# Moving three groups of matmul operands by 64 to 224 bytes in SBUF: a two-block transformer forward pass on one core

## The chip, the core and the metric

The program runs on one core of one Trainium2 chip. The metric is device time in microseconds (us) for one launch. Three runs of the kernel before gave 4149.29, 4153.81 and 4155.1 us; the median, 4153.81 us, is the time before.

## The reference

Two transformer-like blocks follow one another on 256 tokens of width 2048, all in fp32. The first block mixes tokens with two attention branches (a latent-attention branch and a sparse branch with an indexer), the second with an mLSTM and a small state-space model; each then has the same kind of feed-forward part, a product-key memory ("peer"): every token picks 16 of 128 x 128 = 16384 experts per head, for 8 heads.

```python
x = x + merged @ w_out                                   # block 1, after the two branches
x = x + peer_ffn(rmsnorm(x, g), w_q, sub_keys, u, v)     # experts' u and v: 16384 x 2048 each
x = rmsnorm(x, norm_final_g)
...                                                      # block 2: the same frame, another mixer
u = u_emb[expert]
a = gelu(einsum('thkd,td->thk', u, xb))
coef = (softmax(top_scores) * a)
out = einsum('thk,thkd->td', coef, v_emb[expert])
```

## The kernel before

The kernel computes the feed-forward parts densely: all 16384 expert activations are formed by matrix products with all of `u`, multiplied by a gate matrix that is zero where an expert was not picked, and multiplied with all of `v`. Every large product is done in three matmuls of type fp32r, because each operand is split into a high part and a low remainder: high x high, high x low, low x high. `products` (line 231) issues all of them.

A matmul has a stationary operand (`lhsT`, 128 x 128, brought in by a weight load) and a moving operand (`rhs`) that is streamed past it. Two arrangements occur.

- *The U stages* (lines 551 to 570, `cols`): 128 weight tiles of each feed-forward part. The stationary operand is a 128 x 128 piece of `w_hi` or `w_lo`; the moving one is 256 columns of `hT`, the normalised activations, transposed and split (`norm_T`, line 301, writes them and `hT`, line 295, allocates them). 48 matmuls a tile, into `ps_u`. The query projections of both feed-forward parts and most input projections of the two mixers have the same shape.
- *The V stages* (`tile_v`): 128 weight tiles of each feed-forward part. The stationary operand is a piece of `coef_hi` or `coef_lo`, the gated activations; the moving one is 512 columns of `w_hi` or `w_lo`. 24 matmuls a tile, into `ps_v`. Both output projections (`out_proj`) and some input projections (`row_products`, `lead_products`) are of this kind, with a piece of `hT` or `ckvT` as the stationary operand.

Matmuls follow one another without a gap in the work; each weight load runs while the matmul before it streams.

SBUF is handed out by pools, in the order in which `Ctx` opens them: `const`, `small`, `state`, `weights`, `pairs` from the bottom, and two pools from the top (`side="right"`), `pad3` and `hT`; each stage opens its own pool (`mix1`, `route`, `mix2`) above `pairs`. In the program before, the tiles of interest begin at these bytes of each partition; what counts below is the remainder by 512, the length of one weight load's row (128 columns of 4 bytes).

| tile | begins at byte | by 512 |
|---|---|---|
| `w_hi`, four buffers | 67584, 71680, 75776, 79872 | 0 |
| `w_lo`, four buffers | 83968, 88064, 92160, 96256 | 0 |
| `coef_hi`, `coef_lo` (pool `pairs`) | 100352, 102400; 104448, 106496 | 0 |
| stage pools (`mix1`, `route`, `mix2`) | 108544 | 0 |
| `cqT`, `o_hi`, `o_lo` (pool `mix1`, behind its own pad of 32 bytes) | between 108576 and 141344 | 32 |
| `ckvT` (pool `mix1`) | 160832 | 64 |
| `hT` with shift 8 (input of both mixers and both feed-forward parts) | 196096 + 32 | 32 |
| `hT` with shift 0 (output projections) | 196096 | 0 |

All steps from one matmul of a tile to the next are multiples of 512 bytes for a stationary operand and of 1024 or 2048 for a moving one (`in_kv` and `in2_v` with their 272 and 344 columns apart), so the remainder of a tile holds for every matmul that reads it.

DMA loads go through SP's queue into `w_raw`, ScalarE (ACT) makes `w_hi`, VectorE (DVE) and in part GpSimd (POOL) make `w_lo`. Side work (routing, attention, the state-space model) is threaded between weight tiles by `step`.

Of the kernel before, what the change touches and what calls it, by code (L numbers as in the profile page):

```python
# [7 lines left out]
F32, F32R, F16, U32, I32 = dt.float32, dt.float32r, dt.float16, dt.uint32, dt.int32  # L8
# [4 lines left out]
P = 128  # L13
T = 256
TB = 2
D = 2048
KD = D // P
# [5 lines left out]
class Halves:  # L23


    def __init__(self, tiles, h):
        self.tiles, self.h = tiles, h
# [6 lines left out]
class Ctx:  # L34


    def __init__(self, ctx, tc):
        self.tc, self.nc = tc, tc.nc
        nc = self.nc
        pool = lambda name, bufs, **kw: ctx.enter_context(tc.tile_pool(name=name, bufs=bufs, **kw))  # L40
        self.const = pool("const", 1)
        self.small = pool("small", 1)
        self.state = pool("state", 1)
        self.wp = pool("weights", 2)
        self.two = pool("pairs", 2)
        self.pad3 = pool("pad3", 1, side="right")
        self.top = pool("hT", 1, side="right")
        nc.gpsimd.memset(self.pad3.tile([P, 112], F32, name="pad"), 0.0)
        self.ps = pool("psum", 2, space=bass.MemoryType.PSUM)
        it = self.const.tile([P, P], F32, name="iota_f")  # L50
        nc.gpsimd.iota(it, pattern=[[1, P]], base=0, channel_multiplier=-1,
                       allow_small_or_imprecise_dtypes=True)
        self.diff = it
        self.ident = self.const.tile([P, P], F32, name="ident")
        nc.vector.tensor_scalar(self.ident, it, 0.0, None, op0=OP.is_equal)
        self.iota = self.const.tile([P, P], F16, name="iota_h")
        nc.gpsimd.iota(self.iota, pattern=[[1, P]], base=0, channel_multiplier=0,
                       allow_small_or_imprecise_dtypes=True)
        self.half_pi = self.const.tile([P, 1], F32, name="half_pi")
        nc.vector.memset(self.half_pi, float(np.pi / 2))  # L60
        self.x = self.state.tile([P, TB, D], F32, name="x")
        self.sq = self.small.tile([P, TB, 4], F32, name="x_sq")
        self.sq2 = self.small.tile([P, TB, 4], F32, name="x_sq2")
        self.twice, self.first, self.normed, self.done, self.fused = False, {}, {}, set(), {}
        self.bg = []
        self.late = []
        self.credit = 0.0
        self.fine = 0
        self.last = None
        self.lo = [None, None]  # L70
        self.hold = False
# [222 lines left out]

    def hT(self, shift=8):

        both = self.top.tile([P, 2 * KD * T + 8], F32R, name="hT")[:, shift:shift + 2 * KD * T]
        both = both.rearrange("p (two k t) -> p two k t", two=2, k=KD)
        return both[:, 0], both[:, 1]

    def norm_T(self):

        with self.tc.high_priority(SOON):
            hh, hl = self.hT()
            for tb in range(TB):
                n = self.normed.pop(tb)
                tt = slice(tb * P, (tb + 1) * P)
                for c in range(4):
                    ps = self.ps.tile([P, 4, P], F32, name="ps_v", bufs=4)
                    for j in range(4):  # L310
                        self.nc.tensor.transpose(ps[:, j], n[:, (4 * c + j) * P:(4 * c + j + 1) * P], self.ident)  # L311
                    kk = slice(4 * c, 4 * c + 4)
                    split = self.split(hh[:, kk, tt], hl[:, kk, tt], ps)
        if self.twice:
            def scale():
                for tb in range(TB):
                    with self.behind(split):
                        r = self.rsqrt(self.first[tb], 1.0 / D)
                    for c in range(4):
                        o = self.x[:, tb, c * 512:(c + 1) * 512]  # L320
                        with self.behind(split):
                            self.nc.vector.tensor_scalar(o, o, r, None, op0=OP.mult)
                        yield 0.4

            self.bg.append(scale())
            self.twice = False
        return hh, hl
# [13 lines left out]
def peer(K, wq, keys, u, v, g_out, g_next=None, dst=None, later=None):  # L341
# [8 lines left out]
    nc, ctx = K.nc, ExitStack()  # L350
# [2 lines left out]
    rp = ctx.enter_context(K.tc.tile_pool(name="route", bufs=1))  # L353
    kt = rp.tile([P, keys.shape[1], P], F32, name="keysT", tag="acts", bufs=4)
    nc.gpsimd.dma_start(kt, keys)
    hh, hl = K.norm_T()

    i1T = rp.tile([P, T], F32, name="i1T")
    i2T = rp.tile([P, T], F16, name="i2T")
# [1443 lines left out]
def program(tc, I, out):  # L1803
    with ExitStack() as ctx:
        K = Ctx(ctx, tc)
        dram = s5_dram(K, ctx)
        mix1(K, I)
        peer(K, I["p1_q"], I["p1_k"], I["p1_u"], I["p1_v"], I["norm_final_g"], g_next=I["norm1_g"],
             later=s5_prepare(K, I, dram))
        mix2(K, I, dram)  # L1810
        peer(K, I["p2_q"], I["p2_k"], I["p2_u"], I["p2_v"], I["final_g"], dst=out)
# [14 lines left out]
```

## Time and profile before

| | |
|---|---|
| median of 3 runs | 4153.81 us (4149.29 to 4155.1) |
| the profiled execution, its own time | 4154.97 us |
| its span, first to last instruction | 4153.2 us |
| TensorE (PE) busy | 4087.2 us, 98% of the span |
| VectorE, ScalarE, GpSimd busy | 67%, 49%, 38% |
| mean granted TensorE clock | 0.993 of full speed |

In views of the engine's time, "PE" are matmuls and "PEld" the weight loads that run under them. The duration that a matmul row shows (some 280 ns for 256 columns) is longer than the step to the next one, since matmuls are pipelined; the rate has to be read from the difference of two start times, divided by the number of matmuls between them.

### The profile page before, as it was taken

How to read it: one execution, taken by the hardware profiler on the slowest of the kernel's cores; microseconds unless marked ns; L12 is line 12 of the kernel's file. 1: busy time of each engine (PE TensorE's matmuls, PEld its weight loads, DVE VectorE, ACT ScalarE, POOL GpSimd, SP SyncE). 2: the span in 40 equal slices, each digit the busy share in tenths (PEclk: the TensorE clock that was granted, in tenths of full speed). 3: DMA queues.
4: the chain of work that ended last, by engine and by line, in shares of the span. 5: the costliest groups of instructions: out<-in, count | busy, mean ns of one | idle time of the engine just before them, and what ended most of it. 6: DMA issues, size and time to landing. Idle time of an engine off the chain costs nothing. (4 is left out here: it accounts for less than half of the span.)

```text
span 4153.2 us, 74559 instructions
## 1 busy us (share of the span) xinstructions
PE 4087.2 (98%) x29233; PEld 3780.5 (91%) x29233; DVE 2789.2 (67%) x4644; ACT 2019.0 (49%) x2842; POOL 1595.4 (38%) x1322
## 2 busy tenths in 40 slices
PE   8999999999999999999999999999999999999998
PEld 7999989999887899988879998999998889999887
DVE  6775558977767766676567665787765556665565
ACT  5565444444554444444553565444445544444554
POOL 1100015877105477742015542677720017771000
PEclk9999999999999999999999999999999999999999
DMA  5445554555656655566658545555555555555564
GB/s 180 162 152 184 188 180 156 173 191 176 195 191 217 198 177 181 178 217 214 205 183 263 179 149 174 179 170 175 178 183 193 195 192 181 179 177 189 193 204 164
DMA packets 234163, 769.97 MB, mean 185 GB/s; under 512 B 44305, under 2 KB 46353, under 8 KB 233042
## 3 DMA queue, kind: packets, MB, share of 16 engines
q1 hardware_dynamic: 227906, 742.96, 54.5%
q0 software_dynamic: 5904, 22.25, 1.4%
q8 instruction: 229, 3.75, 0.4%
q14 instruction: 124, 1.01, 0.1%
HBM read 748.85 MB, written 16.25 MB: 184 GB/s over the span
## 5 line engine op out<-in xcount | busy, mean ns | idle before, releaser
L222 DVE TENSOR_TENSOR w_lo<-w_raw,w_hi 128x1024 fp32r<-128x1024 f32 (+3 forms) x1308 | 1616.3, 1269 | 1150.8 <-issue 884.5
L216 ACT CAST w_hi<-w_raw 128x1024 fp32r<-128x1024 f32 (+1 forms) x1388 | 1446.9, 1045 | 1586.8 <-PE ps_v L231 625.5
L231 PE MATMUL ps_u<-hT,w_hi 128*128 128x256 f32 x11424 | 1426.3, 281 | 3.2 <-DVE gate L1479 1.7
L231 PEld LDWEIGHTS ps_u<-hT,w_hi 128*128 128x128 f32 x11424 | 1368.8, 188 | 6.3 <-DVE gate L1479 2.0
L504 POOL TENSOR_SCALAR oh<-iota_h,i1T 128x128 f16<-128x128 f16 x896 | 972.4, 1104 | 691.4 <-PE ps_v L231 379.7
L231 PE MATMUL ps_u<-hT,w_lo 128*128 128x256 f32 x5712 | 731.5, 280 | 7.8 <-POOL w_lo L220 6.6
L231 PEld LDWEIGHTS ps_u<-hT,w_lo 128*128 128x128 f32 x5712 | 695.2, 188 | 9.7 <-POOL w_lo L220 7.6
L231 PE MATMUL ps_v<-w_hi,coef_lo 128*128 128x512 f32 x2048 | 693.5, 391 | 6.9 <-DVE coef_lo L271 6.9
L231 PE MATMUL ps_v<-w_hi,coef_hi 128*128 128x512 f32 x2048 | 689.6, 390 | 0.0
L231 PE MATMUL ps_v<-w_lo,coef_hi 128*128 128x512 f32 x2048 | 512.9, 389 | 0.0
L231 PEld LDWEIGHTS ps_v<-w_hi,coef_lo 128*128 128x128 f32 x2048 | 384.5, 188 | 87.9 <-DVE coef_lo L271 8.3
L231 PEld LDWEIGHTS ps_v<-w_hi,coef_hi 128*128 128x128 f32 x2048 | 385.0, 188 | 80.0
L231 PEld LDWEIGHTS ps_v<-w_lo,coef_hi 128*128 128x128 f32 x2048 | 384.2, 188 | 79.8
L220 POOL TENSOR_TENSOR w_lo<-w_raw,w_hi 128x1024 fp32r<-128x1024 f32 (+3 forms) x161 | 304.3, 1903 | 231.8 <-PE ps_u L231 137.3
L270 ACT CAST coef_hi<-acts 128x512 fp32r<-128x512 f32 x256 | 159.4, 624 | 185.2 <-PE ps_v L231 180.2
L271 DVE TENSOR_TENSOR coef_lo<-acts,coef_hi 128x512 fp32r<-128x512 f32 x256 | 188.3, 736 | 0.8 <-ACT coef_hi L270 0.8
L118 POOL TENSOR_TENSOR normed<-x,gain 128x512 f32<-128x512 f32 x22 | 37.8, 1739 | 360.5 <-DVE x L95 273.8
L231 PE MATMUL ps_v<-w_hi,hT 128*128 128x512 f32 (+2 forms) x576 | 126.7, 370 | 1.5 <-ACT hT L270 1.1
L231 PEld LDWEIGHTS ps_v<-w_hi,hT 128*128 128x128 f32 x576 | 101.0, 190 | 20.4 <-ACT hT L270 1.3
L1240 POOL TENSOR_TENSOR s_prm<-s_bc,s_prm 128x512 f32<-128x512 f32 x16 | 26.3, 1641 | 234.6 <-DVE s_prm L1207 234.1
L107 POOL DMA_DIRECT2D gain<-in_final_g x1 | 0.6, 593 | 252.7 <-DVE coef_lo L271 252.7
L513 DVE TENSOR_TENSOR rh<-oh,g_hi 128x512 f16<-128x512 f16 x128 | 94.5, 738 | 0.1
(485 smaller groups left out, 3217.4 us busy)
## 6 DMA issues: line engine op xcount, KB each, us to landing
w_raw<-in_p_u SPq DMA_DIRECT2D x512, 512.0 KB, 4.2
w_raw<-in_p_v SPq DMA_DIRECT2D x512, 512.0 KB, 4.3
w_raw<-in_in_gates SPq DMA_DIRECT2D x64, 512.0 KB, 4.0
w_raw<-in_w_out SPq DMA_DIRECT2D x64, 512.0 KB, 3.9
w_raw<-in_p_q SPq DMA_DIRECT2D x48, 512.0 KB, 4.2
w_raw<-in_in_t SPq DMA_DIRECT2D x38, 512.0 KB, 4.0
w_raw<-in_w_ab SPq DMA_DIRECT2D x32, 512.0 KB, 4.2
w_raw<-in_in_qk SPq DMA_DIRECT2D x32, 512.0 KB, 3.8
```

The costliest lines, as they stand in the source:

```text
L107: self.nc.gpsimd.dma_start(gb, bass.AP(tensor=g.tensor, offset=g.offset, ap=[[0, P], [1, D]]))
L118: eng.tensor_tensor(self.normed_cols(tb, c), self.x[:, tb, cc], gb[:, cc], op=OP.mult)
L216: nc.scalar.copy(hi[i], raw[i])
L220: self.lo[1] = nc.gpsimd.tensor_tensor(lo[i][:, m:], raw[i][:, m:], hi[i][:, m:].bitcast(F32), op=OP.subtract)
L222: self.lo[0] = nc.vector.tensor_tensor(lo[i][:, :m], raw[i][:, :m], hi[i][:, :m].bitcast(F32), op=OP.subtract)
L231: self.last_mm = self.nc.tensor.matmul(out, lhsT=a, rhs=b, start=start, stop=stop)
L270: self.nc.scalar.copy(hi, src)
L271: return self.nc.vector.tensor_tensor(lo, src, hi.bitcast(F32), op=OP.subtract)
L504: one = e.tensor_scalar(oh1[:, t], K.iota, i1T[:, t0 + t:t0 + t + 1], None, op0=OP.is_equal)
L513: nc.vector.tensor_tensor(rh, oh2, b2(gh), op=OP.mult)
L1240: e.tensor_tensor(tm, aa(1), zz(1 - part), op=OP.mult)
```

## The change

A second pad of 64 bytes, in a pool of its own, is opened between `weights` and `pairs`. The pad at the top shrinks from 448 to 224 bytes, and the `hT` tile grows by the same 224 bytes, so that its start stays at byte 196096. `norm_T` takes the shift as an argument: both mixers keep 8 (32 bytes), the feed-forward part of block 1 uses 32 (128 bytes) and that of block 2 uses 64 (256 bytes).

```diff
         self.wp = pool("weights", 2)
+        self.pad2 = pool("pad2", 1)
         self.two = pool("pairs", 2)
...
-        nc.gpsimd.memset(self.pad3.tile([P, 112], F32, name="pad"), 0.0)
+        nc.gpsimd.memset(self.pad3.tile([P, 56], F32, name="pad"), 0.0)
+        nc.gpsimd.memset(self.pad2.tile([P, 16], F32, name="pad2"), 0.0)
...
     def hT(self, shift=8):
-        both = self.top.tile([P, 2 * KD * T + 8], F32R, name="hT")[:, shift:shift + 2 * KD * T]
+        both = self.top.tile([P, 2 * KD * T + 64], F32R, name="hT")[:, shift:shift + 2 * KD * T]
...
-    def norm_T(self):
+    def norm_T(self, shift=8):
...
-            hh, hl = self.hT()
+            hh, hl = self.hT(shift)
...
-    hh, hl = K.norm_T()
+    hh, hl = K.norm_T(32 if dst is None else 64)
```

By the sizes in the code, the remainders by 512 become: weights 0 as before; `coef_hi` and `coef_lo` 64; the stage pools 64, so `cqT`, `o_hi`, `o_lo` 96 and `ckvT` 128; `hT` 32 in the mixers and 0 in the output projections as before, 128 and 256 in the feed-forward parts.

## Rows read from the trace of the kernel before

**Rows 1.** The page's head: span, then busy time of each engine.

```profile
span 4153.2 us, 74559 instructions
...
PE 4087.2 (98%) x29233; PEld 3780.5 (91%) x29233; DVE 2789.2 (67%) x4644; ACT 2019.0 (49%) x2842; POOL 1595.4 (38%) x1322
```

**Rows 2.** Waits of PE: who was waited for, total us, times, longest.

```profile
PE ps_v L311 <- DVE normed L146: 21.9, 5, 8.2
...
PE ps_v L231 <- DVE hT L271: 0.5, 1, 0.5
```

**Rows 3.** The chain of work, pieces in order of time: start, us, what.

```profile
3069.84 348.20 PE ps_v L231 x1536
```

**Rows 4.** Groups of PE by shape: count | busy us, mean ns | idle before.

```profile
L231 PE MATMUL ps_u<-hT,w_hi 128*128 128x256 f32 x11424 | 1426.3, 281 | 3.2 <-DVE gate L1479 1.7 <-ACT acts L568 1.5
L231 PE MATMUL ps_u<-hT,w_lo 128*128 128x256 f32 x5712 | 731.5, 280 | 7.8 <-POOL w_lo L220 6.6 <-DVE w_lo L222 1.2
L231 PE MATMUL ps_v<-w_hi,coef_lo 128*128 128x512 f32 x2048 | 693.5, 391 | 6.9 <-DVE coef_lo L271 6.9
```

**Rows 5.** Timeline of PE, output projection of block 1, `hT` at 0: start, us.

```profile
544.20 3.79 PE L231 MATMUL ps_v<-w_hi,hT 128*128 128x512 f32 x16
547.83 1.98 PE L231 MATMUL ps_v<-w_lo,hT 128*128 128x512 f32 x8
549.64 3.79 PE L231 MATMUL ps_v<-w_hi,hT 128*128 128x512 f32 x16
```

**Rows 6.** Timeline of PE, first input projection, `hT` at 32.

```profile
40.94 3.90 PE L231 MATMUL ps_g<-w_hi,hT 128*128 128x512 f32 x16
44.67 2.03 PE L231 MATMUL ps_g<-w_lo,hT 128*128 128x512 f32 x8
46.54 0.67 PE L231 MATMUL ps_v<-w_hi,hT 128*128 128x272 f32 x4
```

**Rows 7.** Timeline of PE around the products with `ckvT`, at 64.

```profile
104.72 0.63 PE L231 MATMUL ps_v<-w_hi,ckvT 128*128 128x512 f32 x2
...
107.29 0.40 PE L231 MATMUL ps_v<-w_lo,ckvT 128*128 128x512 f32 x1
107.53 0.63 PE L231 MATMUL ps_u<-ckvT,w_hi 128*128 128x256 f32 x4
...
108.70 0.39 PE L231 MATMUL ps_u<-ckvT,w_lo 128*128 128x256 f32 x2
108.94 1.20 PE L231 MATMUL ps_v<-w_lo,ckvT 128*128 128x512 f32 x4
```

**Rows 8.** Timeline of PE in a U stage of block 2, moving `hT` at 32.

```profile
3452.61 3.90 PE L231 MATMUL ps_u<-hT,w_hi 128*128 128x256 f32 x32
3456.34 2.03 PE L231 MATMUL ps_u<-hT,w_lo 128*128 128x256 f32 x16
3458.21 0.20 PE L520 MATMUL ps_g<-rh,oh 128*128 128x64 f16 x1
```

**Rows 9.** Timeline of PE, 256 columns of weights moving, stationary `hT` at 32.

```profile
68.84 3.95 PE L231 MATMUL ps_v<-w_hi,hT 128*128 128x256 f32 x32
72.63 2.06 PE L231 MATMUL ps_v<-w_lo,hT 128*128 128x256 f32 x16
74.52 0.60 PE L807 MATMUL ps_g<-ident,normed 128*128 128x128 f32 x4
```

**Rows 10.** Windows, a V and a U stage: us, each engine's busy us, PEclk, DMA, GB/s.

```profile
3070.00:3418.00 348.00, 348.00 (x1538) 288.14 (x1537) 194.42 (x201) 172.56 (x190) 5.25 (x6) 1.00 0.58 193
3418.00:3794.00 376.00, 376.00 (x3582) 374.69 (x3581) 239.77 (x329) 168.89 (x273) 253.75 (x251) 1.00 0.55 180
```

**Rows 11.** Timeline of POOL at the start.

```profile
0.73 0.19 POOL L48 MEMSET pad<- 128x112 f32 x1 [0.29 <-POOLq L1819]
...
13.83 2.34 POOL L220 TENSOR_TENSOR w_lo<-w_raw,w_hi 128x1024 fp32r<-128x1024 f32 x1 [10.00 <-ACT w_hi L216]
```

## The prediction

> **What bounds the kernel now.** I read the page's head first: TensorE is busy for 4087 of the 4153 us, the next engine for 67% [rows 1]. A busy share close to one can still hide waits, so the waits of PE come next: the longest in total is 21.9 us, for the normalised tiles, and all fifteen rows, of which the first and the last are shown, sum to 55.5 us [rows 2]. Then the chain of work: through a V stage it is one piece, 1536 matmuls in 348.20 us with nothing between them [rows 3]. Such a stage ends when PE has got through its matmuls, and the windows say that nothing else could be the limit there: VectorE is busy for 194 of 348 us and ScalarE for 173, at full granted clock [rows 10]. So what counts is the step from one matmul to the next. A row's own duration (390 ns) doesn't tell it, since matmuls overlap; the difference of two start times does.
>
> The change adds no matmul, no transfer and no wait. It changes where operands begin. The question is therefore whether the step depends on that, and the trace of before holds comparisons for it, since its stages already use different starts.
>
> **512 columns moving, the V stages.** Three cases, all with weights moving from remainder 0 (by 512 bytes) and only the start of the stationary operand different:
> - stationary at 0. V stage: 348.20 / 1536 = 0.2267 us [rows 3]. Output projection, where `hT` is stationary with shift 0: 24 matmuls from 544.20 to 549.64, 5.44 / 24 = 0.2267 us [rows 5]. Two different tiles at quite different addresses, one step.
> - stationary at 32. First input projection: 24 matmuls from 40.94 to 46.54, 5.60 / 24 = 0.2333 us [rows 6].
> - stationary at 64. The products with `ckvT`: 12 matmuls from 104.72 to 107.53, 2.81 / 12 = 0.234 us [rows 7].
>
> So the same work costs 6.6 to 7 ns more per matmul when the weight load does not begin at the same remainder as the stream above it. That VectorE, ScalarE or the DMA traffic cause it is unlikely: the V stage holds its 226.7 ns over 348 us under changing traffic. The change puts `coef_hi` and `coef_lo` at 64, with weights still at 0: exactly the case of `ckvT`. I take the longer run's 6.6 ns. Matmuls of this kind: three groups of 2048, of which one row is shown, the other two being `coef_hi` with `w_hi` and `w_lo` [rows 4], so 6144. Term: 6144 x 6.6 ns = +40.6 us. Bounds: nothing (if the twelve matmuls with `ckvT` and the run at 32 don't speak for a long V stage), and 7.3 ns (234 against 226.7), +45 us. A gain I exclude for the likeliest case, since no 512-column step in the rows is shorter than 226.7 ns.
>
> **256 columns moving, the U stages.** Here `hT` moves and weights are stationary at 0. Now: 48 matmuls from 3452.61 to 3458.21, 5.60 / 48 = 116.7 ns with `hT` at 32 [rows 8]. Half of a V step is 113.3 ns, which I take as the floor for 256 columns. So the present start already costs 3.4 ns, and there is room both ways. The change puts `hT` at 128 (block 1) and 256 (block 2); no row has these. The nearest:
> - moving at 64, stationary at 0: 12 matmuls with `ckvT` from 107.53 to 108.94, 1.41 / 12 = 117.5 ns [rows 7];
> - moving at 0, stationary at 32: 48 matmuls from 68.84 to 74.52, 5.68 / 48 = 118.3 ns [rows 9].
>
> My reading of the five cases: a weight load reads 512 bytes while the stream above it reads 1024, so the stream overtakes the load once per 512 bytes of difference. With equal starts this falls on the boundary between two matmuls and costs nothing; with the stream 32 ahead it falls close to the boundary and costs half; farther inside it costs more. That the two reads disturb each other at equal remainders is inferred from these steps, not seen. By it 128 and 256 lie well inside. I take the mean of the two nearest rows, 117.9 ns, +1.2 ns. Number of matmuls: 17136 with `hT` moving [rows 4], less those of the mixers, which keep 32: 51 tiles in block 1 (19 and 32) and 30 in block 2 (6, 8 and 16), 81 x 48 = 3888. That leaves 13248. Term: 13248 x 1.2 ns = +15.9 us. Bounds: the floor, -3.4 ns, -45 us; and the full V penalty on top of the floor, 113.3 + 6.6 = 119.9 ns, +3.2 ns, +42 us.
>
> **The rest.** `o_hi` and `o_lo` move from 32 to 96 in 768 matmuls of 256 columns, `cqT` in 144: 912 x 1.2 ns = +1.1 us, bounds -3 and +3 us by the same ends. The input projections with `ckvT` or the feed-forward `hT` as the stationary operand were off 0 before and stay off 0: nothing, within 1 us (some 200 matmuls by 5 ns). Shifted starts for VectorE, ScalarE and GpSimd: nothing; those engines have time to spare in both kinds of stage [rows 10], and every start stays a multiple of 32 bytes. The third memset on POOL (the old one took 0.19 us) lies in front of 10 us in which POOL idles [rows 11]; without that cover it would cost 0.1 us. The instructions' order is laid out ahead by estimated times, and that memset could shift it: I take nothing, the bound being a few us of the waits of [rows 2].
>
> **The sum.** 40.6 + 15.9 + 1.1 = +57.6 us. The profiled execution took 4154.97 us, so it would take 4212.6 us; that execution lies 1.2 us above the median, so the median goes from 4153.8 to 4211 us, 1.4% slower.
>
> **Rivals.**
> 1. *The starts do nothing.* This kernel's operands all begin at multiples of 32 bytes, and the steps of 226.7 and 233.3 ns could differ for another cause (other PSUM banks, the neighbouring work). Against it: the steps follow the start of the stationary operand through four stages. Time 4154 us, no change. [...]
> 2. *The V stages pay, the U stages reach the floor.* If 128 and 256 keep the two reads apart instead of letting them meet, U goes to 113.3 ns: +40.6 - 45 - 3 = -7, time 4147 us; half way to the floor it would be 4171 us. For it: the present 116.7 is between floor and worst, so the curve is not flat. Against: 64 is no better than 32.
> 3. *The other sign: the V penalty does not come.* The products with `ckvT` and the first projection have their high and low stationary pieces in one tile; `coef_hi` and `coef_lo` lie in two, as before. If that sets the penalty and not the start, V stays at 226.7 ns, and with U at the floor the time is 4154 - 45 - 3 = 4106 us. The point from which it decides: faster than before as soon as U gains more than V loses, that is, with V unchanged any U step below 116.7 ns; with V at 233.3 ns only below 113.6 ns. Against it: `hT` at 0 also has both pieces in one tile and runs at 226.7 ns [rows 5].
> 4. *Both pay in full.* U at 119.9 ns: +40.6 + 42 + 3, 4240 us.
> 5. *V unchanged, U pays:* 4171 us.
>
> [...]
>
> **How the numbers follow.** Chances: the forecast (V pays, U between no change and +2.5 ns) 0.52; rival 4 0.10; rival 2 0.13, spread from 4147 to 4185 us; rival 3 0.15; rival 5 0.05; rival 1 0.05. A measurement of this kernel can tell about 0.2%, 8.3 us. Slower by more: the forecast, rivals 4 and 5, and a little over a third of rival 2, 0.72. Faster by more: rival 3, and the deepest end of rival 2 by 0.03, 0.18. Within: rival 1 and the remainder of rival 2, 0.10. Given V pays and U doesn't gain, the time lies between 4195 (U unchanged) and 4240 us. The range has to leave out no more than 2 in 10: from 4145, which takes in rivals 1, 2 and 5, to 4243 us, which takes in most of rival 4; rival 3 is left out.
>
> **What the profile after would show.** V: a chain piece of 1536 `ps_v` matmuls of 358 us in place of 348.20, and 24 matmuls of a tile in 5.60 us. U: 48 matmuls in 5.66 us, and the two blocks may differ. Output projections still 5.44 us for 24, mixers' inputs still 5.60 us for 48, since their starts stay. The forecast is wrong if the V step is still 226.7 ns, or if the U step falls to 113 or 114 ns.

## The result, and the profile after

The changed kernel takes 4225.1 us (median of 4 runs, 4219.9 to 4226.5) against 4153.7 us for the kernel before (4 runs): a ratio of 1.0167, with a 95% interval of 1.0155 to 1.0179. The prediction was 4211 us, from 4145 to 4243. Direction and mechanism (a longer step from matmul to matmul, no new wait) hold; the size is 71 us, not 57.

The profiled execution of after took 4226.47 us, with a span of 4224.7 us. The page's head, to be read beside [rows 1] (all lines of the program are two numbers further on, 231 is now 233):

```profile
span 4224.7 us, 74560 instructions
...
PE 4161.3 (99%) x29233; PEld 3816.8 (90%) x29233; DVE 2780.3 (66%) x4644; ACT 2014.6 (48%) x2842; POOL 1576.4 (37%) x1323
```

PE has the same 29233 instructions and is busy for 74.1 us longer, while the span grew by 71.5. So the time is inside PE's own work. Its waits confirm it: they sum to 52.9 us against the 55.5 us of [rows 2], the longest 7.6 us against 8.2. Two of the rows:

```profile
PE ps_v L313 <- DVE normed L148: 21.2, 5, 7.6
PE ps_u L233 <- POOL w_lo L222: 5.7, 3, 3.1
```

The chain of work holds the same unbroken V piece as [rows 3], 10.2 us longer:

```profile
3111.22 358.40 PE ps_v L233 x1536
```

358.40 / 1536 = 233.3 ns per matmul against 226.7. The groups by shape, as in [rows 4], show the same from the other end: equal counts, and a mean duration that rose from 281 to 284 ns in the U kind and from 391 to 397 in the V kind:

```profile
L233 PE MATMUL ps_u<-hT,w_hi 128*128 128x256 f32 x11424 | 1450.0, 284 | 3.8 <-DVE gate L1481 2.3
...
L233 PE MATMUL ps_v<-w_hi,coef_lo 128*128 128x512 f32 x2048 | 705.7, 397 | 7.4 <-DVE coef_lo L273 5.4
```

The timeline of PE in places that the change does not touch: the first input projection (`hT` at 32, as in [rows 6]), 256 columns of weights over a stationary `hT` ([rows 9]), and an output projection (`hT` at 0, [rows 5]). 24 matmuls take 5.60 us, 48 take 5.69 and 24 take 5.44, as before within 0.01 us. The products with `ckvT` ([rows 7]), also shown here, are touched: their start goes from 64 to 128. Their 12 matmuls of 512 columns take 2.78 us (2.81 before), the 12 of 256 columns behind them 1.43 us (1.41 before).

```profile
40.49 3.90 PE L233 MATMUL ps_g<-w_hi,hT 128*128 128x512 f32 x16
44.22 2.03 PE L233 MATMUL ps_g<-w_lo,hT 128*128 128x512 f32 x8
46.09 2.18 PE L233 MATMUL ps_v<-w_hi,hT 128*128 128x272 f32 x16
...
68.39 3.95 PE L233 MATMUL ps_v<-w_hi,hT 128*128 128x256 f32 x32
72.18 2.06 PE L233 MATMUL ps_v<-w_lo,hT 128*128 128x256 f32 x16
74.08 0.60 PE L809 MATMUL ps_g<-ident,normed 128*128 128x128 f32 x4
...
104.42 0.62 PE L233 MATMUL ps_v<-w_hi,ckvT 128*128 128x512 f32 x2
...
107.20 0.63 PE L233 MATMUL ps_u<-ckvT,w_hi 128*128 128x256 f32 x4
...
108.63 1.09 PE L233 MATMUL ps_v<-w_lo,ckvT 128*128 128x512 f32 x4
...
541.03 3.79 PE L233 MATMUL ps_v<-w_hi,hT 128*128 128x512 f32 x16
544.66 1.98 PE L233 MATMUL ps_v<-w_lo,hT 128*128 128x512 f32 x8
546.47 3.79 PE L233 MATMUL ps_v<-w_hi,hT 128*128 128x512 f32 x16
```

And in the U stages, which it does touch: a tile of block 1 (`hT` at 128), then one of block 2 (at 256), each followed by the next work.

```profile
1572.16 3.96 PE L233 MATMUL ps_u<-hT,w_hi 128*128 128x256 f32 x32
1575.95 2.06 PE L233 MATMUL ps_u<-hT,w_lo 128*128 128x256 f32 x16
1577.86 0.20 PE L522 MATMUL ps_g<-rh,oh 128*128 128x64 f16 x1
...
3547.64 4.00 PE L233 MATMUL ps_u<-hT,w_hi 128*128 128x256 f32 x32
3551.48 2.08 PE L233 MATMUL ps_u<-hT,w_lo 128*128 128x256 f32 x16
3553.40 0.20 PE L522 MATMUL ps_g<-rh,oh 128*128 128x64 f16 x1
```

48 matmuls take 5.70 us at 128 (118.8 ns) and 5.76 us at 256 (120.0 ns); in [rows 8] it was 5.60 (116.7). The windows that answer to [rows 10] have PE busy throughout (348.00 of 348.00 and 370.00 of 370.00 us) at full granted clock (1.00), and the other engines with as much room as before (VectorE 187.02 us against 194.42 in the V window):

```profile
3112.00:3460.00 348.00, 348.00 (x1493) 280.41 (x1492) 187.02 (x192) 168.18 (x186) 0.00 (x0) 1.00 0.56 188
3470.00:3840.00 370.00, 370.00 (x3450) 368.62 (x3449) 232.82 (x323) 161.27 (x265) 252.44 (x250) 1.00 0.53 174
```

The split memset on POOL, [rows 11], costs nothing, as forecast: the work behind the gap starts at 13.39 instead of 13.83 us.

```profile
0.73 0.14 POOL L49 MEMSET pad<- 128x56 f32 x1 [0.29 <-POOLq L1821]
0.81 0.11 POOL L50 MEMSET pad<- 128x16 f32 x1
...
13.39 2.34 POOL L222 TENSOR_TENSOR w_lo<-w_raw,w_hi 128x1024 fp32r<-128x1024 f32 x1 [9.55 <-ACT w_hi L218]
```

Where the 71 us lie, from the start times of the first matmul of each stage in the two traces:

| part | before, us | after, us | more |
|---|---|---|---|
| start to the first V stage | 1061.8 | 1066.8 | 5.0 |
| block 1, V (first) | 364.5 | 374.4 | 9.9 |
| block 1, U | 375.8 | 382.2 | 6.4 |
| block 1, V (second) | 372.1 | 380.8 | 8.7 |
| second mixer, queries, first U of block 2 | 895.4 | 906.9 | 11.5 |
| block 2, V (first) | 348.2 | 358.4 | 10.2 |
| block 2, U | 376.5 | 386.3 | 9.8 |
| block 2, V (second) | 348.0 | 358.2 | 10.2 |

V stages: 39.0 us, forecast 40.6. All the rest: 32.7 us, forecast 17.0.

### The profile page after: what moved, and what is told of

Same layout as the page of the kernel before. It is cut to its first block, busy times and chain, and to the rows that moved or that the text cites. A ratio compares the mean times of both kernels' runs of the same rounds, so it can differ in the third digit from the quotient of the medians.

```text
span 4224.7 us, 74560 instructions
## 1 busy us (share of the span) xinstructions
PE 4161.3 (99%) x29233; PEld 3816.8 (90%) x29233; DVE 2780.3 (66%) x4644; ACT 2014.6 (48%) x2842; POOL 1576.4 (37%) x1323
## 5 line engine op out<-in xcount | busy, mean ns | idle before, releaser
L233 PE MATMUL ps_u<-hT,w_hi 128*128 128x256 f32 x11424 | 1450.0, 284 | 3.8 <-DVE gate L1481 2.3
L233 PEld LDWEIGHTS ps_u<-hT,w_hi 128*128 128x128 f32 x11424 | 1391.8, 190 | 6.8 <-DVE gate L1481 2.5
L506 POOL TENSOR_SCALAR oh<-iota_h,i1T 128x128 f16<-128x128 f16 x896 | 941.7, 1068 | 753.9 <-PE ps_v L233 393.0
L233 PE MATMUL ps_u<-hT,w_lo 128*128 128x256 f32 x5712 | 742.7, 282 | 5.8 <-POOL w_lo L222 5.7
L233 PEld LDWEIGHTS ps_u<-hT,w_lo 128*128 128x128 f32 x5712 | 706.6, 190 | 7.5 <-POOL w_lo L222 7.0
L233 PE MATMUL ps_v<-w_hi,coef_lo 128*128 128x512 f32 x2048 | 705.7, 397 | 7.4 <-DVE coef_lo L273 5.4
L233 PE MATMUL ps_v<-w_hi,coef_hi 128*128 128x512 f32 x2048 | 702.1, 396 | 0.0
L233 PE MATMUL ps_v<-w_lo,coef_hi 128*128 128x512 f32 x2048 | 526.3, 396 | 0.0
```

The source lines that it names most:

```text
L233: self.last_mm = self.nc.tensor.matmul(out, lhsT=a, rhs=b, start=start, stop=stop)
L506: one = e.tensor_scalar(oh1[:, t], K.iota, i1T[:, t0 + t:t0 + t + 1], None, op0=OP.is_equal)
```

## The experiments

In all of them "offset" is the start of the moving operand less the start of the stationary one, in bytes. A step is the mean time from one matmul's start to the next one's within a stage, in that run's trace; steps across other work are left out. Times of the experiments are medians where there is more than one run.

**Each half alone.** The first keeps only the 64 bytes in front of `coef`, `o_hi` and their like, the second only the new starts of `hT`:

```
v_only:  +   self.pad2 = pool("pad2", 1)
         +   nc.gpsimd.memset(self.pad2.tile([P, 16], F32, name="pad2"), 0.0)
u_only:      pad3 [P, 112] -> [P, 56];  hT [.. + 8] -> [.. + 64]
             norm_T() -> norm_T(32 if dst is None else 64)   # as in the change
```

> Only the 64-byte pad between the weights and the pairs: coef at 64, the stage pools at 64, hT as before. Theory (the step depends on where the weight load begins relative to the stream above it, by 512 bytes): V step 233.3 ns, U step 116.8 ns as before, 912 matmuls with o_hi, o_lo and cqT at 96 some 3 ns longer; 4155 + 41 + 3 = 4198 us. Rival (the two moves of the change need each other): V step stays at 226.7 ns and the time at 4154 us.

> Only hT at 128 and 256 in the feed-forward parts, no pad, coef at 0. Theory: V step 226.7 ns; U step 118.8 ns in block 1 and 120.0 ns in block 2, as in the changed kernel: 6432 x 2.0 + 6816 x 3.2 ns = 35 us more, 4189 us. Rival (U is longer because coef, acts and the routing tiles moved): U stays at 116.8 ns, 4154 us.

`v_only` took 4191.8 us (ratio 1.0096, interval 1.0076 to 1.0116), `u_only` 4182.3 us (1.0073, 1.0053 to 1.0093). 39.5 and 30.0 us more than the kernel before beside them (4152.4): together 69.4 of the 71.4. Each is 6 to 7 us short of what was expected, though the steps came out as expected. The chain pieces of block 2's first V stage, `v_only` and then `u_only`, and a tile of its second U stage in the same two runs show that each half acts only where its operands are used:

```profile
3086.13 358.40 PE ps_v L233 x1536
```

```profile
3085.93 348.19 PE ps_v L231 x1536
```

```profile
3550.32 3.90 PE L233 MATMUL ps_u<-hT,w_hi 128*128 128x256 f32 x32
3554.06 2.03 PE L233 MATMUL ps_u<-hT,w_lo 128*128 128x256 f32 x16
3555.93 0.20 PE L522 MATMUL ps_g<-rh,oh 128*128 128x64 f16 x1
```

```profile
3554.61 4.00 PE L231 MATMUL ps_u<-hT,w_hi 128*128 128x256 f32 x32
3558.45 2.08 PE L231 MATMUL ps_u<-hT,w_lo 128*128 128x256 f32 x16
3560.37 0.20 PE L520 MATMUL ps_g<-rh,oh 128*128 128x64 f16 x1
```

48 matmuls take 5.61 us in `v_only`, about the 5.60 of [rows 8], and 5.76 us in `u_only`, as in after.

**All starts moved by the same 64 bytes.** As the prediction has it, only the difference between the two starts counts. Here the pad stands in front of the weights' pool too, so that weights, `coef` and `o_hi` begin 64 bytes later, and every `hT` does as well:

```
+   self.pad2 = pool("pad2", 1)          # in front of "weights", not of "pairs"
    norm_T() -> norm_T(24)  everywhere;  K.hT(0) -> K.hT(16)   # 4-byte elements: 32 -> 96, 0 -> 64
```

> Weights, coef, stage pools and every hT (the output projections' too) begin 64 bytes later than before, so that nothing moves relative to the weights. Theory (relative starts count): V step 226.7 ns, U step 116.8 ns, time as before, 4154 us within 3. Rival (absolute starts count: a stationary row that does not begin at a multiple of 512 bytes is dearer): V step 233.3 ns and U step 118 to 120 ns, 4195 to 4235 us.

4153.4 us, ratio 1.0004 (0.9991 to 1.0017): no change, with V at 226.7 and U at 116.8 ns. Its V piece:

```profile
3066.84 348.18 PE ps_v L233 x1536
```

So in this run neither 64 as such nor the added pad cost anything; what counted was a start against the other operand's.

**Equal starts.** The prediction's reading said that equal starts cost nothing and took 113.3 ns as the floor for 256 columns. By the period of 512 that it assumed, the change never sets them equal in a U stage, so this was run by itself:

```
    norm_T() -> norm_T(0)   everywhere (nothing else changed)
```

> hT at 0 in both mixers and both feed-forward parts, coef at 0 as before: every large product has equal starts. Theory (equal starts meet on the boundary and cost nothing): the U step falls from 116.8 to 113.3 ns for 17136 matmuls, 59 us less, and the 512-column products of the first mixer fall to 226.7 ns: 4094 us. Rival (with 256 columns the load is as long as the stream, so equal starts meet at both ends): U step 116 to 118 ns or more, 4140 to 4175 us.

4199.8 us, ratio 1.0119 (1.0097 to 1.0142): slower, beyond the rival's times too. My theory failed here for 256 columns; its 512-column half held, with 24 matmuls of the first projection in 5.44 us, 226.7 ns each. A tile of block 2 in its timeline takes 5.76 us, 120.0 ns per matmul, as much as with `hT` at 256 in after:

```profile
3544.12 4.00 PE L231 MATMUL ps_u<-hT,w_hi 128*128 128x256 f32 x32
3547.96 2.08 PE L231 MATMUL ps_u<-hT,w_lo 128*128 128x256 f32 x16
3549.88 0.20 PE L520 MATMUL ps_g<-rh,oh 128*128 128x64 f16 x1
```

**The step over the offset.** Five kernels set `hT` differently in the two mixers and the two feed-forward parts, and `coef` at one more place each:

```
          mixer 1  feed-fwd 1  mixer 2  feed-fwd 2   coef      (bytes)
scan_a       16        48         64        96       128
scan_b      192       160        224       320       256
scan_c      448       384        288       448       320
scan_d      200       208        216       176       240 (lies at 256)
scan_e      184       200        240       216       224
```

> A look at more starts. hT at 16 bytes in mixer 1, 48 in feed-forward 1, 64 in mixer 2, 96 in feed-forward 2; pad of 128 bytes before the pairs, so coef at 128. Theory (only the relative start by 512 counts, and the two kinds of product have different curves): U-like steps of 117 to 120 ns with 64 near the 118 ns of the products with ckvT; V step near 232 ns, as for the 12 products with ckvT at 128 in the changed kernel. Rival (the curve repeats every 256 bytes, since 0 and 256 both gave 120 ns): the same here; the two other looks tell.

> hT at 192 bytes in mixer 1, 160 in feed-forward 1, 224 in mixer 2, 320 in feed-forward 2; coef at 256. Rival (the curve repeats every 256 bytes): U step at 320 the 118.0 ns of 64, V step at 256 the 226.7 ns of 0. Theory (period 512): U steps of 117 to 120 ns with no such twins, V step 231 to 235 ns.

> hT at 448 bytes in mixer 1, 384 in feed-forward 1, 288 in mixer 2, 448 in feed-forward 2; coef at 320. Rival (period 256): U step at 288 the 116.8 ns of 32, at 384 the 118.8 ns of 128, V step at 320 the 233.3 ns of 64. Theory (period 512): no such twins; mixer 1 and feed-forward 2, both at 448, show the same step, since the stage doesn't count.

> A finer scan: hT at 200 in mixer 1, 208 in the feed-forward part of block 1, 216 in mixer 2, 176 in that of block 2; coef_hi and coef_lo at 240, so the weights begin 16 beyond them modulo 256. Theory now: the 256-column step has its low point between 192 and 224, so 113 to 116 ns at 200 and 208, 115 to 118 at 216, 115 to 118 at 176. The 512-column step lies between the 226.7 of 0 and the 229 of 64, 226.5 to 228. Rival (the low readings at 192 and 448 belong to what else runs in those stages, not to the start): no order among the four, all at 116 to 118.

> The same scan at 184 in mixer 1, 200 in the feed-forward part of block 1, 240 in mixer 2, 216 in that of block 2; coef at 224, so the weights begin 32 beyond it modulo 256. Theory now: 200 gives the same step here in the feed-forward part as in mixer 1 of the scan with 200 there, 113 to 116 ns; 216 between 114 and 118; 184 at 114 to 117; 240 at 118 to 120, near the 119.85 of an equal start. The 512-column step 226.7 to 229. Rival: the steps go by the stage and not by the start, and 200 differs by over 1 ns between the two scans.

They took 4219.8, 4160.1, 4177.5, 4196.5 and 4249.1 us, one run each. In `scan_d` the pad of 240 bytes put `coef` at 256: the built program has `coef_hi` at byte 100608, 256 beyond 100352. So it repeats the 256 of `scan_b`, with the same V piece of 348.19 us for 1536 matmuls, and an offset of 16 was not tried for 512 columns. The steps of all runs, with the offset taken modulo 256:

| offset mod 256 | 256 columns, ns | 512 columns, ns |
|---|---|---|
| 0 | 119.9 (`hT` at 0; at 256 in after) | 226.7 (`coef` at 0; at 256) |
| 16 | 117.0 | |
| 32 | 116.7 (before); 116.9 (at 288) | 233.3 (`coef` at 224) |
| 48 | 118.3 | |
| 56 | | 230.5 (first projection, `hT` at 200) |
| 64 | 117.8 (at 64; at 320) | 229.0 (first projection, `hT` at 192; at 448) |
| 72 | | 232.0 (first projection, `hT` at 184) |
| 96 | 120.0 | |
| 128 | 118.9 (at 128; at 384) | 231.7 (`ckvT` in after); 233.3 (`coef` at 128) |
| 160 | 118.0 to 118.7 | |
| 176, 184 | 119.2, 120.0 | |
| 192 | 114.8 (at 192); 113.5 to 115.4 (at 448) | 233.3 (`coef` at 64; at 320) |
| 200, 208, 216 | 120.5, 119.1, 121.1 | |
| 224, 240 | 118.3, 117.2 | 233.2, 233.3 (first projection, `hT` at 32; at 16) |

Three things follow. In the pairs tried the step repeats every 256 bytes, not every 512: 0 and 256, 64 and 320, 128 and 384 agree within 0.2 ns; 192 (114.8 ns) and 448 (113.5 to 115.4) are the two lowest of 256 columns. Its mean goes with the offset more than with the stage: 200 gives 120.6 in a mixer and 120.5 in the other scan's feed-forward part, 216 gives 121.1 in both kinds of stage; at 192 and 448 stages differ by up to 1.9 ns, elsewhere by 0.7 at most. And at two offsets the two widths go opposite ways: 0 is the best of 512 columns (226.7 ns) and among the worst of 256 (119.9), 192 the best of 256 (114.8) and among the worst of 512 (233.3). The finer scan also refuted what I had made of the curve by then, a smooth low point between 192 and 224: the neighbours 184 (120.0 ns) and 200 (120.5) are among the worst, 192 is low by itself (114.8), and 512 columns at an offset of 32, expected at 226.7 to 229 ns, took 233.3.

These are means, and they hide that at one offset an unbroken series of matmuls can keep one of several steps. In the first mixer of `scan_a` (offset 16), two successive tiles with `hT` moving:

```profile
360.67 3.81 PE L233 MATMUL ps_u<-hT,w_hi 128*128 128x256 f32 x32
364.32 1.98 PE L233 MATMUL ps_u<-hT,w_lo 128*128 128x256 f32 x16
366.13 0.28 PE L233 MATMUL ps_v<-o_hi,w_hi 128*128 128x256 f32 x1
...
371.77 3.96 PE L233 MATMUL ps_u<-hT,w_hi 128*128 128x256 f32 x32
375.56 2.06 PE L233 MATMUL ps_u<-hT,w_lo 128*128 128x256 f32 x16
377.46 0.28 PE L233 MATMUL ps_v<-o_hi,w_hi 128*128 128x256 f32 x1
```

The 48 matmuls take 5.46 us, at 113.3 ns after the first steps, and then 5.69 us, at 118.7; such tiles alternate so to the end of that mixer, and earlier series run at 116.7 or 118.7. So the 117.0 in the table is a mixture, and 113.3 ns does not belong to 192 alone. Which steps were seen differs from offset to offset (at 448, below, 113.3 and 117.8 ns); what picks one of them for a series is open.

**`hT` at 448 everywhere, `coef` left at 0.** In the U and V stages both widths have the lowest mean step that was found:

```
    pad3 [P, 112] -> [P, 8];  hT [.. + 8] -> [.. + 112]
    norm_T() -> norm_T(112)   everywhere (448 bytes);  K.hT(0) as before
```

> The weights' pairs stay where they were before the change (coef at 0); the transposed activations hT begin 448 bytes beyond a multiple of 512 in both mixers and both feed-forward parts, the output projections' hT at 0. Theory now (the step follows the moving start less the stationary start, repeating every 256 bytes, with a low point just below a multiple of 256): the 256-column steps go from 116.7 ns to 113.5-115.4 ns, 17136 matmuls x 1.3 to 3.2 ns = 22 to 55 us less, the V stages stay at 226.7 ns: 4099 to 4132 us. Rival 1 (what PE gains comes back as waits, since VectorE's or the weights' pairs then end last): same steps, but 4140 to 4154 us, and the stage of block 2's first products no shorter than before. Rival 2 (the prediction's period of 512, where 448 lies 64 short of an equal start): 116 to 119 ns, 4145 to 4190 us.

4115.6 us against 4154.7, ratio 0.9906 (0.989 to 0.9923): 0.9% shorter, within the times expected, and faster than both kernels. A tile of block 2's U stage takes 5.44 us, 113.3 ns per matmul, in its timeline:

```profile
3552.88 3.79 PE L231 MATMUL ps_u<-hT,w_hi 128*128 128x256 f32 x32
3556.51 1.98 PE L231 MATMUL ps_u<-hT,w_lo 128*128 128x256 f32 x16
3558.32 0.20 PE L520 MATMUL ps_g<-rh,oh 128*128 128x64 f16 x1
```

The page's head shows PE busy for 46.6 us less than in [rows 1], in a span 41.3 us shorter:

```profile
span 4111.9 us, 74559 instructions
...
PE 4040.6 (98%) x29233; PEld 3734.4 (91%) x29233; DVE 2784.8 (68%) x4644; ACT 2019.4 (49%) x2842; POOL 1604.9 (39%) x1322
```

And the V piece of its chain is that of [rows 3]:

```profile
3037.76 348.17 PE ps_v L231 x1536
```

Over a whole stage the step is 113.7 to 114.8 ns. A tile behind the fp16 matmuls is a little longer, 5.54 us from 3547.34 to the 3552.88 at which the tile above begins, against its 5.44; and some series stay at 117.8 ns at this same offset, about one matmul in seven. The stage of the tile above begins with such a series, 5.66 us a tile; after the first fp16 matmuls it runs at 113.3:

```profile
3385.77 3.93 PE L231 MATMUL ps_u<-hT,w_hi 128*128 128x256 f32 x32
3389.54 2.05 PE L231 MATMUL ps_u<-hT,w_lo 128*128 128x256 f32 x16
3391.43 3.93 PE L231 MATMUL ps_u<-hT,w_hi 128*128 128x256 f32 x32
```

Little of what PE gains is eaten by waits: they sum to 60.7 us against 55.5, about the difference between 46.6 and 41.3; the longest is still that for `normed`, 22.6 us in 5 waits.

## Why the prediction was right in direction and short in size

**What bounds the kernel.** Right. PE's waits did not grow (52.9 us against 55.5), and the span followed PE's busy time.

**The V term, +40.6 us.** Right in size, and from the right comparison: `ckvT` at 64 is the same offset, and with `coef` there the step is the 233.3 ns of [rows 6], 39.0 us in the stages and 39.5 in `v_only`. The rule stated with it was too broad: a start that differs by 256 costs nothing (`coef` at 256, 226.7 ns), and at an offset of 64 the price is 2.3 ns and not 6.6. The two block 1 stages pay 9.9 and 8.7 us, not 10.2; they hold other work between their V matmuls (364.5 and 372.1 us before, against 348.2 and 348.0 in block 2), and what takes up the difference was not traced.

**The U term, +15.9 us.** This is the term that was mis-sized. The step was taken as 117.9 ns, the mean of the rows at 64 ([rows 7]) and with weights moving ([rows 9]); it measured 118.9 in block 1 and 119.9 in block 2, +2.2 and +3.2 ns instead of +1.2. By these steps the term is 6432 x 2.2 + 6816 x 3.2 ns = 36 us, 2.7 ns on average, past the +2.5 ns up to which the prediction counted its forecast. Block 2's U stage shows it cleanly: 3072 x 3.2 = 9.8 us, and 9.8 measured; block 1's: 3072 x 2.2 = 6.8, and 6.4 measured. The upper bound that the prediction kept, 119.9 ns, is what block 2 reached: block 2 is rival 4 (both pay in full), block 1 lies between it and the forecast, and so does the whole, 4225 between 4211 and 4240 us. `u_only`, where this term stands alone, took 30.0 us more than before, 25.7 in its trace. There the U stage in the middle of either block pays 6.9 and 9.6 us, as the steps give; the two parts with more side work between the tiles pay less, 2.5 us up to the first V stage (7.4 by the steps) and 6.7 us from block 1's second V stage to block 2's first (12.0).

**The reading behind it.** Refuted for 256 columns, in both of its parts. In the runs the period is 256 and not 512, so a start of 256 counts as an equal start (119.9 ns in after, as at 0 in `hT_zero`); and an equal start is not free but costs those 119.9 ns against the 113.3 taken as the floor. Free equal starts had been read from the 512-column rows, where they hold (226.7 ns, the lowest step there), and carried to 256 columns; the period of 512 came from the lengths of the reads, and no row could show it. It fails for 512 columns too (`coef` at 256, 226.7 ns). The stream that overtakes the load was my own picture, and no run shows it. Had I only counted the period right, the reading would have put block 2 at the floor and given a worse forecast: that block 2 was forecast to pay at all is luck, two errors that cancel. That its 119.9 ns equals the bound built from the floor and the V penalty is explained by no run. The floor of 113.3 ns exists, but at an offset of 192, and in some series at 16.

**The rest, +1.1 us.** By the step of `cqT`, 8 matmuls from 102.26 to 103.22 us in after, 0.96 us where two such series took 0.93 and 0.94 before, the 912 matmuls at 96 pay about 3 ns, 2.8 us. Against that the part up to the first V stage grew by only 5.0 us, where its 3360 U matmuls (x 2.2 = 7.4) and these would give 10.2. Summed from start to start in the two traces, the matmuls with `hT` moving pay 5.3 us there and those with `cqT`, `o_hi` and `o_lo` 2.7, while PE's other work takes 1.0 us less and its waits 1.9 us less. In this part the U step of before was 117.0 ns on average and not 116.7 (some series run at 117.9), so it rose by only 1.9 ns, 6.5 us; the last 1.2 us of the U matmuls are open. `all_64`, with the steps of before, reaches its first V stage 2.6 us earlier too, with waits of 18.3 us there against 22.0: fewer waits also come without any change of an offset.

**The rivals.** 1 (starts do nothing) falls by the steps of every run but `all_64`, which is the one where no offset changes: an offset alone turned 226.7 into 233.3 ns (`v_only`). That it is the two reads that disturb each other fits `all_64` but was my inference and is not shown: no row shows a read. 2 (U at the floor) and 3 (no V penalty) fall by the steps of after, 5 by `v_only`.

## What to carry to other kernels

When PE is the bound, read the step between matmul starts, not the duration of one (391 ns in a V row of before, at a step of 226.7), and compare it across places where the operands begin differently: 3% of a 512-column step and up to 7% of a 256-column step (113.5 against 121.1 ns) hung on it here. Such a price belonged to one width and one offset: at offset 0 the step was the lowest of 512 columns (226.7 ns) and among the highest of 256 (119.9), so taken from another width it had the wrong sign; look or measure before you carry it over. If an allocator decides the starts, treat its padding as a parameter and pin the difference between the two operands, not the address of either: with every start 64 bytes later (`all_64`) the time stayed within a ratio of 1.0004. Then look at the series one by one: a mean over a stage can mix two steps, as the 113.3 and 118.7 ns of `scan_a` in its 117.0.

## What was not expected of the hardware

In these runs the mean step of the matmuls went with the difference of the two operands' starts modulo 256 bytes (119.9 ns at 0 and at 256, 117.8 at 64 and at 320), finely enough that 8 bytes (192 against 200) changed a 256-column step from 114.8 to 120.5 ns. The best place found for 256 columns (192, 114.8 ns) is among the worst for 512 (233.3 ns), and the best for 512 (0, 226.7 ns) cost 119.9 ns at 256. And one offset held two steps, 113.3 and 117.8 ns at 448, each kept through a whole series. What sets the shape between these points, and which step a series takes, is open.
